# Sixty-two idle transposes in place of forty in the opening of a decoder-block kernel

## The chip, the core and the metric

The kernel runs on one core of a Trainium2 chip. The core has a matrix engine (TensorE, "PE" in the profile, its weight loads "PEld"), a vector engine (VectorE, "DVE"), a scalar engine (ScalarE, "ACT"), GpSimd ("POOL") and a sync engine that issues most transfers ("SP"). Each engine works through its own list of instructions in order; semaphores tie the lists together. The metric is the device time of one execution in microseconds, the median over several runs.

## The reference

One decoder layer on x of shape 1024 x 1024, in float32:

```python
u = rms_norm(h, mix_pre_g)
z = einsum('bsd,de->bse', u, w_in)               # p, q, k, v and two gates
ya = pool_mixer(p) @ w_branch_a                  # causal pooling, windows 2, 4, 8, 16
yb = diff_attention(q, k, v) @ w_branch_b        # 4 heads, two softmaxes each
m = sigmoid(gate_a) * ya + sigmoid(gate_b) * yb
h = h + rms_norm(m @ w_out, mix_post_g)
u = rms_norm(h, ffn_pre_g)
f = silu(u @ w_ffn_gate) * (u @ w_ffn_up)        # hidden width 2816
h = h + rms_norm(f @ w_ffn_down, ffn_post_g)
```

## The kernel before

All large products run on TensorE in a reduced float format. Each operand is split into a high part and a low part, and each product is three matmuls: high by high, low by high, high by low. The tiles of the activations are called `A_hi` and `A_lo` in the opening, those of the weights `w_hi` and `w_lo`. After the opening most products are done by a seven-product scheme on half matrices.

The work has four stages: the opening (normalising x and the first q and k products, up to about 80 us), the rest of the input projection, the attention and output projection, and the feed-forward part. Only the opening is touched by the change.

In the opening, x is loaded twice: by rows (tiles `xt`, eight blocks of 512 KB, line 344) for the sums of squares, and already transposed (tiles `xp` and `S_raw`, lines 349 and 353) as the operand of the products. ScalarE squares and sums each row block (line 389). For a group of two blocks VectorE adds the epsilon (line 397), GpSimd raises to the power -1/2 (line 398), and the result `rstd`, one value per row, has to become one value per column: two transposes on TensorE of a broadcast column (line 404, tile `R` in PSUM) do this, the "spreading" of 1/rms. ScalarE or VectorE copies `R` to SBUF (line 408). There are four such groups and so four spreadings. The transposed x is multiplied by the gain (lines 430 and 433), then by `R` (line 303, from `second_stage`), cast to `A_hi` (line 458), and the remainder is `A_lo` (line 1405). The weights are cast to `w_hi` (line 492), and the remainder is `w_lo` (line 1405). Then come the first products, `qk` (line 542), in pairs of matmuls with 256 moving columns.

Before x arrives TensorE has nothing to do. Line 318 issues 10 transposes of the identity matrix into a PSUM tile `warm` that nobody reads, as one task, and lines 320 to 322 issue 40 more, each a task of its own.

The order of the work within each engine of the opening is fixed by a planner in the kernel's own code (class `Plan`), when the program is built. Each task has an engine, a cost in us as its author wrote it, its tiles and a rank. The planner walks through planned time: on each engine it takes, among the tasks that can start at once, the one with the smallest rank. The idle transposes have rank 1,000,000, so one of them is put in only where no other TensorE task is ready in the plan. They are chained to each other since all write the tile `warm`. The plan fixes only the order; on the chip each instruction runs when the one before it on its engine and the semaphores it waits for allow it. TensorE starts in the plan at 1.42, the planner charges 0.11 when TensorE resumes after idling, and a result of GpSimd reaches TensorE 0.15 after its end, one of ScalarE 0.10 after its end.

Of the kernel before, what the change touches and what calls it, by code (L numbers as in the profile page):

```python
# [16 lines left out]
P = 128  # L17
# [226 lines left out]

AIM = 34.641
WARM0 = 10
WARM1 = 40
FORMS = (("DVE", "DVE", "DVE", "DVE",), ("DVE", "DVE", "DVE", "DVE",),)
WBEHIND = (0, None, 0, None,)
WSPLIT = (0, 1, 1, 0,)  # L250
# [30 lines left out]
def opening(pl, k):  # L281

    nc = k.nc if k else None
# [9 lines left out]
    def bank(pool, s):  # L293
        return pl.tile(pool, lambda: getattr(k, pool)(s))

    def small(n, s):
        return pl.tile("small", lambda: k.small(n, s))
# [11 lines left out]
    for g, w in enumerate(WINDOWS):  # L309
# [3 lines left out]
              w=[cnt], rank=-50)  # L313
# [3 lines left out]
    bw = bank("mm", "warm")  # L317
    pl.op("PE", WARM0 * .213, lambda: [nc.tensor.transpose(bw()[:, i % 4 * P:(i % 4 + 1) * P], k.ident, k.ident)
                                       for i in range(WARM0)], w=[bw], rank=-2000)
    for i in range(WARM1):  # L320
        pl.op("PE", .109, lambda i=i: nc.tensor.transpose(bw()[:, i % 4 * P:(i % 4 + 1) * P], k.ident, k.ident),
              w=[bw], rank=1e6)
    early = small(1, "early")
    pl.op("ACT", 1.3, lambda: A.copy(early(), k.mhalf[:, :1]), w=[early], rank=-2999)
    gk = small(KD, "gk")
# [44 lines left out]
    for c in LOADS:  # L370
        if c < 10:
            load_x(c)
        elif c < 20:
            i = c - 10
# [9 lines left out]
    for gi, grp in enumerate(GROUPS):  # L384
        n = len(grp)
        ss, r = small(n, "ss"), small(n, "rstd")
        for j, tb in enumerate(grp):
# [4 lines left out]
            else:  # L392
# [6 lines left out]
              rank=RT[gi], port=True)  # L399
# [84 lines left out]
    for i in range(4):  # L484
# [16 lines left out]
        else:  # L501
            pl.op("DVE", 1.23, lambda i=i: k.sub(wl[i](), view(i), wh[i]()), r=[raw[i], wh[i]],
                  w=[(wl[i], c) for c in range(4)], rank=WRANK[i] + 1, port=True)

    U = {"A11": AT[0, 0], "A12": AT[0, 1], "A22": AT[1, 1]}
    for n, raw_ in (("S1", s1), ("S2", r11), ("S3", s3), ("S4", r12)):
# [3 lines left out]
              rank=SRANK[n] + .5, port=True)  # L510
# [847 lines left out]
def block_kernel(ctx, tc, x, w_in, pool_mix, pool_scale, w_branch_a, lam_q1, lam_k1, lam_q2,  # L1358
# [203 lines left out]
    def qk_done(h, e, t, src, st):  # L1562
# [16 lines left out]
    lamt = temp("sg").rearrange("p (i d) -> p i d", d=HD)  # L1579
    first = Plan()  # L1580
    U, W, st = opening(first, SimpleNamespace(
        nc=nc, a8=a8, b4=b4, mm=mm, fil=fil, pair=pair, small=small, wp=wp, name=name, f32=f32, triple=triple, temp=temp,
        sub=sub, junk=junk, mhalf=mhalf, ident=ident, cnt=cnt, x=x, xt0=xt0, xt1=xt1, gk=gk, wqk=wqk, qd=qd, kd=kd, AF=AF))
# [393 lines left out]
```

## Time and profile before

| | us |
|---|---|
| median of 3 runs | 1244.17 (1243.64 to 1244.72) |
| the profiled execution, its own time | 1243.25 |
| span of the profiled execution | 1241.5 |
| TensorE busy | 1230.6 (99%) |
| VectorE busy | 842.7 (68%) |
| ScalarE busy | 584.2 (47%) |
| GpSimd busy | 127.8 (10%) |

The span runs from the first to the last instruction of the program; 1.75 us of the execution's own time lie around it. In a timeline row the first number is the start in us, the second how long the group lasted, then engine, line, operation, tiles, shape and count; in square brackets stands how long the engine had idled and what ended this. In a row of a table by stretches of time each engine has its busy time and its count of instructions, and "PEclk" is the granted share of the TensorE clock.

### The profile page before, as it was taken

The page shows a single profiled execution, that of the slowest core. Times are in us where ns is not written, and L with a number is a line of the kernel's source. Part 1 is how long each engine was busy: PE and PEld are TensorE (multiplying, and loading weights), DVE is VectorE, ACT ScalarE, POOL GpSimd, SP SyncE. Part 2 cuts the span into 40 slices and gives each one's busy share as a digit, 9 for nine tenths or more (in the row PEclk, how much of TensorE's full clock was granted, in tenths as well). Part 3 has the DMA queues.
Part 4 walks back from the last instruction along what each step waited for, and adds up shares of the span by engine and source line. Part 5 has one row for each costly group of instructions (what it writes and reads, how often), then busy time and mean ns, then how long its engine had stood idle before and what let it go on. Part 6 is the DMA issues. An engine that isn't in the chain of part 4 may idle for free.

```text
span 1241.5 us, 15579 instructions
## 1 busy us (share of the span) xinstructions
PE 1230.6 (99%) x5838; PEld 1033.0 (83%) x5838; DVE 842.7 (68%) x1307; ACT 584.2 (47%) x1049; POOL 127.8 (10%) x108
## 2 busy tenths in 40 slices
PE   8999999999999999999999999999999999999998
PEld 8888888888899998888888888888888888888886
DVE  6986784534599888886895564565655547955666
ACT  8643444443588773454643333333333333554542
POOL 1000000000201110011001111101111102000222
PEclk9999999999999999999999999999999999999999
DMA  9665346323783028562523232232332368733236
GB/s 372 234 196 185 108 152 226 124 80 118 289 321 136 18 86 290 195 243 94 191 89 120 93 127 102 94 102 95 117 127 86 125 215 276 233 103 100 81 106 212
DMA packets 133820, 194.36 MB, mean 157 GB/s; under 512 B 7920, under 2 KB 82416, under 8 KB 131312
## 3 DMA queue, kind: packets, MB, share of 16 engines
q1 hardware_dynamic: 126928, 172.26, 40.8%
q10 hardware_dynamic: 6816, 21.11, 4.4%
q8 instruction: 46, 0.75, 0.2%
q14 instruction: 30, 0.25, 0.1%
HBM read 131.73 MB, written 61.60 MB: 156 GB/s over the span
## 4 chain that ended last, share of the span: by engine, by line
PE 97%; DMA 1%; DVE 1%; ACT 0%; issue 0%; POOLq 0%; POOL 0%; DVEq 0%; ACTq 0%
PE Y L1498 10%; PE Y L1500 10%; PE Y L1499 10%; PE X L1498 5%; PE X L1500 5%; PE X L1499 5%; PE qk L542 4%; PE Yd L1498 3%; PE Yd L1500 3%; PE Yd L1499 3%; PE Z L1500 3%; PE Z L1498 3%; PE Z L1499 3%; PE s L710 3%; PE o L710 3%; PE wo L1500 2%
## 5 line engine op out<-in xcount | busy, mean ns | idle before, releaser
L1449 DVE TENSOR_TENSOR p<-Z,p 128x512 f32<-128x512 f32 x32 | 22.1, 691 | 160.7 <-PE Z L1500 160.7
L1498 PE MATMUL X<-S_hi,Wh 128*128 128x512 f32 x288 | 112.3, 390 | 0.0
L1498 PE MATMUL Y<-S_hi,Wh 128*128 128x512 f32 x288 | 112.2, 390 | 0.0
L1499 PE MATMUL Y<-S_lo,Wh 128*128 128x512 f32 x288 | 112.2, 389 | 0.0
L1500 PE MATMUL Y<-S_hi,Wl 128*128 128x512 f32 x288 | 112.1, 389 | 0.0
L1499 PE MATMUL X<-S_lo,Wh 128*128 128x512 f32 x288 | 112.1, 389 | 0.0
L1500 PE MATMUL X<-S_hi,Wl 128*128 128x512 f32 x288 | 112.0, 389 | 0.0
L1498 PE MATMUL Y<-A_hi,Wh 128*128 128x512 f32 x280 | 109.1, 390 | 0.0
L1499 PE MATMUL Y<-A_lo,Wh 128*128 128x512 f32 x280 | 109.1, 390 | 0.0
L1500 PE MATMUL Y<-A_hi,Wl 128*128 128x512 f32 x280 | 109.0, 389 | 0.0
L1467 ACT CAST Wh<-wf_t 128x1024 fp32r<-128x1024 f32 x62 | 64.3, 1052 | 64.1 <-PE Y L1499 32.8
L1405 DVE TENSOR_TENSOR Wl<-wf_t,Wh 128x1024 fp32r<-128x1024 f32 x72 | 87.6, 1223 | 6.1 <-ACT Wh L1467 4.6
L1405 DVE TENSOR_TENSOR w_op<-wd,w_op 128x512 fp32r<-128x512 f32 x77 | 56.6, 735 | 51.4 <-ACT w_op L1453 51.4
L1453 ACT CAST w_op<-wd 128x512 fp32r<-128x512 f32 x77 | 47.9, 622 | 78.0 <-PE Yd L1500 35.1
L1467 ACT CAST Wh<-w_raw 128x1024 fp32r<-128x1024 f32 (+1 forms) x62 | 51.9, 837 | 63.1 <-PE Z L1499 38.3
L1405 DVE TENSOR_TENSOR Wl<-w_raw,Wh 128x1024 fp32r<-128x1024 f32 x72 | 68.6, 953 | 15.0 <-ACT Wh L1467 13.6
L1498 PE MATMUL Yd<-w_op,s_op 128*128 128x512 f32 x176 | 68.6, 390 | 0.0
L1499 PE MATMUL Yd<-w_op,s_op 128*128 128x512 f32 x176 | 68.5, 389 | 0.0
L1500 PE MATMUL Yd<-w_op,s_op 128*128 128x512 f32 x176 | 68.3, 389 | 0.0
L1498 PEld LDWEIGHTS Y<-S_hi,Wh 128*128 128x128 f32 x288 | 54.1, 188 | 11.6 <-ACT u L1540 0.5
L1500 PEld LDWEIGHTS X<-S_hi,Wl 128*128 128x128 f32 x288 | 54.1, 188 | 11.2
L1500 PEld LDWEIGHTS Y<-S_hi,Wl 128*128 128x128 f32 x288 | 54.1, 188 | 11.2
(294 smaller groups left out, 3018.9 us busy)
## 6 DMA issues: line engine op xcount, KB each, us to landing
s_raw<-fsd SPq DMA_DIRECT2D x35, 512.0 KB, 3.5
w_raw<-in_w_in_dram SPq DMA_DIRECT2D x24, 512.0 KB, 4.0
w_raw<-in_w_ffn_gate_dram SPq DMA_DIRECT2D x22, 512.0 KB, 3.7
w_raw<-in_w_ffn_up_dram SPq DMA_DIRECT2D x22, 512.0 KB, 3.7
fsd<-fss SPq DMA_DIRECT2D x11, 1024.0 KB, 3.8
wd<-in_w_ffn_down_dram SPq DMA_DIRECT2D x44, 256.0 KB, 5.2
fsd<-F SPq DMA_DIRECT2D x33, 256.0 KB, 2.2
sgs<-sgd SPq DMA_DIRECT2D x16, 512.0 KB, 8.1
```

The source lines that it names most:

```text
L542: nc.tensor.matmul(o()[:, cs], l, r, start=first and kk == 2 * kh and j == 0, stop=last and kk == 2 * kh + 1 and j == len(todo) - 1, skip_ ...
L710: nc.tensor.matmul(o, l, r, start=start, stop=stop, skip_group_check=skip)
L1405: nc.vector.tensor_tensor(out=o, in0=a, in1=f32(hi), op=ALU.subtract)
L1449: nc.vector.tensor_tensor(out=o, in0=a, in1=b, op=op)
L1453: nc.scalar.copy(hi, a)
L1467: nc.scalar.copy(hi, a)
L1498: nc.tensor.matmul(o, ah, bh, start=start, stop=False, skip_group_check=goes_on)
L1499: nc.tensor.matmul(o, ah, bl, start=False, stop=False, skip_group_check=goes_on)
L1500: nc.tensor.matmul(o, al, bh, start=False, stop=stop, skip_group_check=goes_on)
```

## The change

The number of idle transposes after the first ten goes from 40 to 62. The planner's cost for the first 19 of them goes from 0.109 to 0.161, and each has a rank of its own, growing by one. Nothing else is edited; the planner places the transposes anew.

```diff
-WARM1 = 40
+WARM1 = 62
...
     for i in range(WARM1):
-        pl.op("PE", .109, lambda i=i: nc.tensor.transpose(bw()[:, i % 4 * P:(i % 4 + 1) * P], k.ident, k.ident),
-              w=[bw], rank=1e6)
+        pl.op("PE", .161 if i < 19 else .109, lambda i=i: nc.tensor.transpose(bw()[:, i % 4 * P:(i % 4 + 1) * P], k.ident, k.ident),
+              w=[bw], rank=1e6 + i)
```

## The prediction

> **What bounds the kernel.** I read first the page's busy times and its chain, then who TensorE waited for over the whole span.
>
> ```profile
> span 1241.5 us, 15579 instructions
> ...
> PE 1230.6 (99%) x5838; PEld 1033.0 (83%) x5838; DVE 842.7 (68%) x1307; ACT 584.2 (47%) x1049; POOL 127.8 (10%) x108
> ```
>
> ```profile
> PE qk L542 <- ACT A_hi L458: 2.9, 2, 1.8
> PE warm L318 <- POOL ident masks.py:199: 1.4, 1, 1.4
> PE branch L1498 <- DVE sgs L713: 0.2, 1, 0.2
> ```
>
> TensorE is the bound, and after its first products it waits for nothing but 0.2 us. So the end moves by what TensorE gains or loses in the opening, unless an operand there comes too late. The timeline of the first 21 us shows how the opening goes:
>
> ```profile
> 1.42 2.40 PE L318 MATMUL warm<-ident 128*128 128x128 f32 x10 [1.42 <-POOL ident masks.py:199]
> 3.60 6.20 PE L321 MATMUL warm<-ident 128*128 128x128 f32 x40
> 7.50 0.71 POOL L398 TENSOR_TENSOR rstd<-ms,mhalf 128x2 f32<-128x2 f32 x1 [5.85 <-DVE ms L397]
> 8.63 1.14 DVE L433 TENSOR_SCALAR A_raw<-xp,gk 128x256 f32<-128x256 f32 x4 [1.22 <-DMA xp<-in_xt_dram]
> 9.64 0.38 PE L404 MATMUL R<-ident,rstd 128*128 128x128 f32 x2
> 10.06 0.37 ACT L408 COPY R<-R 128x256 f32<-128x256 f32 x1 [1.01 <-PE R L404]
> 10.46 2.43 DVE L303 TENSOR_TENSOR A_raw<-A_raw,R 128x512 f32<-128x512 f32 x3 [0.69 <-ACT R L408]
> 11.19 1.22 ACT L458 CAST A_hi<-A_raw 128x512 fp32r<-128x512 f32 x2 [0.24 <-DVE A_raw L303]
> 11.86 1.11 PE L542 MATMUL qk<-A_hi,w_hi 128*128 128x256 f32 x4 [1.84 <-ACT A_hi L458]
> 12.98 1.04 ACT L458 CAST A_hi<-A_raw 128x1024 fp32r<-128x1024 f32 x1
> 14.07 1.22 PE L542 MATMUL qk<-A_hi,w_hi 128*128 128x256 f32 x4 [1.11 <-ACT A_hi L458]
> 16.44 1.22 DVE L1405 TENSOR_TENSOR A_lo<-A_raw,A_hi 128x1024 fp32r<-128x1024 f32 x1
> 17.82 1.08 POOL L398 TENSOR_TENSOR rstd<-ms,mhalf 128x2 f32<-128x2 f32 x1 [9.61 <-DVE ms L397]
> 18.14 3.30 ACT L430 ACTIVATE A_raw<-xp,gk 128x256 f32<-128x256 f32 x8
> 19.15 1.84 PE L542 MATMUL qk<-A_lo,w_hi 128*128 128x256 f32 x14
> 20.82 0.38 PE L404 MATMUL R<-ident,rstd 128*128 128x128 f32 x2
> ```
>
> Two things cost time here. The first spreading starts at 9.64, though its input was ready at 7.50 + 0.71 = 8.21: the idle transposes stand in front of it. And the clock falls, as the tables by stretches show (the first for the tile `warm` alone, the second for TensorE):
>
> ```profile
> 3.60:7.00 3.40, 3.40 (x17) 3.40 (x17) 1.00 1.01 396
> 7.02:9.60 2.58, 2.58 (x25) 2.54 (x24) 1.00 0.96 360
> ```
>
> ```profile
> 0.18:3.59 3.41, 2.17 (x10) 1.00 0.49 139
> 3.59:7.01 3.42, 3.42 (x18) 1.00 1.00 395
> 7.01:10.42 3.41, 3.01 (x28) 1.00 0.96 366
> 10.42:13.83 3.41, 1.01 (x4) 1.00 1.05 417
> 13.83:17.25 3.42, 3.17 (x15) 0.50 1.03 412
> 17.25:20.66 3.41, 3.41 (x30) 1.00 1.02 408
> ```
>
> Less the one that reaches in from before, 16 transposes start in 3.40 us (0.213 each) until 7.0, and 24 in 2.58 (0.108 each) after it: TensorE runs at half speed until 7.0, whatever PEclk says there. Between 13.83 and 17.25, one stretch of 3.42 us, the granted clock is 0.50, after a stretch in which TensorE was busy 1.01 of 3.41 us, and 15 matmuls start in it against 30 in the next.
>
> **The change part by part. Where the transposes go** follows from the planner's rule and the costs in the code; it is an order, not a time. In the plan 1/rms is ready for TensorE at 8.14: 0.76 for the issue of the second x block, 2 x 1.30 for two loads of 0.494 MB at 0.38, 2.40 latency, 1.25 for the square, 0.15 and 0.70 for lines 397 and 398, and 0.04, 0.09 and 0.15 for the hand-overs. The forty of before end in the plan at 1.42 + 2.13 + 40 x 0.109 = 7.91, all ahead of the spreading. Now nineteen end at 3.55 + 19 x 0.161 = 6.61, and 15 more start before 8.14 (the last at 8.135), so 34 stand ahead of the spreading, which ends at 8.244 + 0.218 = 8.462. The first pair of products is ready in the plan at 10.63, the second at 11.25, as before, since VectorE's earlier work and not `R` sets them. So (10.63 - 8.462) / 0.109 gives 20 transposes, then a pair (0.24), then 4, a pair, and the last 4, which end at 11.99; the third pair stays at 12.95. From there the plan is the old one, so no other order changes: 34, 20, 4 and 4.
>
> **The spreading.** Six fewer transposes ahead of it, all of them in the fast stretch: 6 x 0.109 = 0.66, so it starts at 8.98, still after 8.21. The copy of `R` moves from 10.06 to 9.40 and VectorE's product from 10.46 to 9.80; VectorE is free at 8.63 + 1.14 = 9.77, so all 0.66 pass. The casts after it move along, and the third pair goes from 14.07 to 13.41.
>
> **The 28 between.** They cost 28 x 0.109 = 3.05 us of TensorE, in time that was idle (9.86 to 11.86, and after the second pair). From 9.20 the 20 end at 11.38. The first pair is ready at about 11.80 - 0.66 + 0.05 = 11.19, and so 0.19 late; nobody waits for it but TensorE. Pair (0.24), 4 (0.44), pair, 4: they end at 12.74, 0.67 before the third pair is ready. Nothing on the path.
>
> **The clock.** From 10.42 to 13.83 TensorE is then busy 2.32 + 0.42 = 2.74 of 3.41 us, 80%, where 1.01 (30%) was followed by the half clock and 3.01 (88%) was not. I take it that the clock stays. Then 15 matmuls take 0.120 in place of 0.213: 15 x 0.093 = 1.40, and about 0.15 for the slower first ones. With it TensorE is 0.66 + 1.5 = 2.2 us ahead at 20.82. The bounds of this term are 0 (clock falls again) and 1.5. The operands of this part allow it: the last `A_lo`, 16.44 + 1.22 - 0.66 = 17.00, is wanted at 19.63 - 2.2 = 17.4, and 1/rms of the second group, at 18.90 - 0.66 = 18.24, at 18.6.
>
> **What is late next.** The timeline further on:
>
> ```profile
> 23.39 1.06 ACT L389 ACTIVATE junk<-xt 128x1024 bf16<-128x1024 f32 x1 [0.91 <-DMA xt<-in_x_dram]
> 24.67 1.06 ACT L389 ACTIVATE junk<-xt 128x1024 bf16<-128x1024 f32 x1
> 25.95 1.06 ACT L389 ACTIVATE junk<-xt 128x1024 bf16<-128x1024 f32 x1
> 27.01 1.03 ACT L458 CAST A_hi<-A_raw 128x1024 fp32r<-128x1024 f32 x1
> 28.07 1.22 DVE L1405 TENSOR_TENSOR A_lo<-A_raw,A_hi 128x1024 fp32r<-128x1024 f32 x1 [0.77 <-ACT A_hi L458]
> 28.46 0.38 PE L404 MATMUL R<-ident,rstd 128*128 128x128 f32 x2
> 28.60 0.72 PE L542 MATMUL qk<-A_hi,w_hi 128*128 128x256 f32 x4
> 29.16 0.38 PE L404 MATMUL R<-ident,rstd 128*128 128x128 f32 x2
> ```
>
> ```profile
> 25.00:28.40 3.40, 3.40 (x31) 1.00 1.03 410
> ```
>
> ScalarE waits for a block of x at 23.39, and the next two squares follow at 1.28 us, which is 512 KB at 410 GB/s: the transfers set these, and the change does not touch them. The cast of 27.01 stands behind the last square in ScalarE's list and ends at 28.04. Of the four matmuls of the row at 28.60, the last two (about 28.92) read its tile. So TensorE cannot pass 28.09 there, and of the 2.2 us only 28.92 - 28.09 = 0.83 is kept; some 1.4 us turn into a new wait for `A_hi`. After it TensorE is 0.83 ahead to the end. VectorE's `A_lo` at 28.07 doesn't move and ends at 29.29, wanted at 31.04 - 0.83.
>
> **The sum**, against the profiled execution: 1243.25 - 0.83 = 1242.42, of which 1241.5 - 0.83 = 1240.7 is span. The median of the runs is 0.92 above the profiled execution: 1244.17 - 0.83 = 1243.3. A difference of 0.2%, about what a measurement of this kernel can tell from no change, is 2.49 us here.
>
> **The rivals.** *No gain.* The clock's stretches are 3.41 us long, and one trace shows only one position of them. Where they lie so that no stretch is nearly idle, the kernel before keeps its full clock, reaches 28.09 by itself, and nothing is gained: 1244.2. The 1.08 us between the three runs speak for such differences; against it, the profiled execution had the half clock and was the fastest of the four. By the Trainium skill, "TensorE: Matmul & The Clock Gate", Part 1, the window is 3413 ns and free-running; the 3.41 of the trace agrees, a second position no run shows yet.
>
> *The transposes don't hold the clock.* Then 13.83 to 17.25 is at half clock again: from 13.41 four matmuls start fast and 16 slowly, 20 against 15, which is 5 x 0.120 = 0.60 ahead, below the 0.83: 1243.6. Against it speaks that the transposes' own spacing halved at 7.0, after a stretch of nothing else. The same page, Part 4, says of transposes that the full clock "doesn't engage" for them; by that rule the time would be this rival's, and the trace does not agree.
>
> *The full gain.* If the wait at 28.09 is not hard, 2.2 us remain: 1242.0. Only earlier transfers of x could do it; the row of 25.00 to 28.40 shows them at 410 GB/s without a pause.
>
> *Slower.* The new wait of 1.4 us, from 26.7 to 28.09, leaves 2.0 of 3.41 us busy (59%) if it lies within one stretch. If that is too little, the next 3.41 us go at half clock and cost 1.71: 1244.17 - 0.83 + 1.71 = 1245.05. It decides if the share at which the clock falls lies above 59%; the trace puts it between 30% and 88%. That 2.17 of 3.41 us (64%) from 0.18 to 3.59 did not raise the clock speaks for it. Against it: to fall and to rise need not have one limit.
>
> **How the numbers follow.** The forecast 0.55, no gain 0.12, the clock not held 0.08, the full gain 0.08, slower 0.12, and 0.05 for something else, such as an order that I worked out wrongly. The predicted time is 1243.3. The range takes in the full gain and the slower rival: 1242.0 to 1245.1. None of the named cases alone passes 2.49 us; faster by over 0.2% takes the full gain and a better position of the stretches (0.06), slower by over 0.2% takes the fallen clock and one more such loss, or the something else (0.07). That leaves 0.87 for within 0.2%.
>
> **What would show it.** In the profile of the changed kernel: the spreading of line 404 near 8.98 with 34 transposes of line 321 ahead of it and 28 behind; granted clock 1.00 from 13.83 to 17.25; the third pair near 13.41; a new wait of `qk` for `A_hi` of line 458 of about 1.4 us that ends near 28.1; the total of the waits of `qk` near 0.67 + 1.4. The prediction is wrong if TensorE's matmul after that wait starts earlier than 28.0 or if the clock falls after it, or if the order behind the third pair differs from before.

## The result, and the profile after

| us | before | changed |
|---|---|---|
| median, 22 runs each | 1244.03 (1242.42 to 1245.38) | 1242.01 (1241.38 to 1242.97) |
| the profiled execution, its own time | 1243.25 | 1242.02 |
| its span | 1241.5 | 1240.2 |

The ratio of the changed kernel to the one before is 0.9985, with a 95% interval of 0.9979 to 0.9991. That is within 0.2%, but it is a gain: 2.02 us between the medians, where 0.83 was forecast. Between the two profiled executions it is 1.23.

The page and the waits of TensorE in the changed kernel (engine, line, waited for: us in total, times, longest):

```profile
span 1240.2 us, 15622 instructions
...
PE 1231.4 (99%) x5860; PEld 1034.7 (83%) x5860; DVE 844.6 (68%) x1307; ACT 584.1 (47%) x1049; POOL 126.8 (10%) x108
```

```profile
PE warm L318 <- POOL ident masks.py:199: 1.4, 1, 1.4
PE qk L542 <- ACT A_hi L458: 1.0, 2, 0.5
PE branch L1498 <- DVE sgs L713: 0.2, 1, 0.2
```

TensorE has its 22 transposes more, and the wait for `A_hi` has shrunk from 2.9 to 1.0 us. Its timeline in the opening:

```profile
3.60 5.57 PE L321 MATMUL warm<-ident 128*128 128x128 f32 x34
9.01 0.38 PE L404 MATMUL R<-ident,rstd 128*128 128x128 f32 x2
9.23 2.35 PE L321 MATMUL warm<-ident 128*128 128x128 f32 x20
11.33 0.48 PE L542 MATMUL qk<-A_hi,w_hi 128*128 128x256 f32 x2
11.65 0.60 PE L321 MATMUL warm<-ident 128*128 128x128 f32 x4
12.01 0.48 PE L542 MATMUL qk<-A_hi,w_hi 128*128 128x256 f32 x2
12.33 0.60 PE L321 MATMUL warm<-ident 128*128 128x128 f32 x4
13.45 0.74 PE L542 MATMUL qk<-A_hi,w_hi 128*128 128x256 f32 x4 [0.52 <-ACT A_hi L458]
18.82 0.38 PE L404 MATMUL R<-ident,rstd 128*128 128x128 f32 x2
26.46 0.38 PE L404 MATMUL R<-ident,rstd 128*128 128x128 f32 x2
26.59 0.48 PE L542 MATMUL qk<-A_hi,w_hi 128*128 128x256 f32 x2
27.57 0.50 PE L542 MATMUL qk<-A_hi,w_hi 128*128 128x256 f32 x2 [0.49 <-ACT A_hi L458]
```

The order is 34, 20, 4 and 4. With the transposes left out, the order on all five engines is that of before. The third pair starts at 13.45 in place of 14.07, the second spreading at 18.82 in place of 20.82, and the pair at 28.92 now starts at 27.57 behind a new wait. TensorE by the clock's stretches (the columns: length, busy us and count of TensorE, PEclk, DMA share, GB/s):

```profile
10.48:13.89 3.41, 2.89 (x26) 1.00 1.05 420
13.89:17.30 3.41, 3.41 (x31) 1.00 1.03 410
```

In the stretch that was followed by the half clock TensorE is now busy 2.89 of 3.41 us, and the half clock is gone.

### The profile page after: what moved, and what is told of

The parts are those of the page before. It is cut to its first block, busy times and chain, and to the rows that moved or that the text cites. A ratio compares the mean times of both kernels' runs of the same rounds, so it can differ in the third digit from the quotient of the medians.

```text
span 1240.2 us, 15622 instructions
## 1 busy us (share of the span) xinstructions
PE 1231.4 (99%) x5860; PEld 1034.7 (83%) x5860; DVE 844.6 (68%) x1307; ACT 584.1 (47%) x1049; POOL 126.8 (10%) x108
## 4 chain that ended last, share of the span: by engine, by line
PE 95%; DMA 3%; DVE 1%; ACT 1%; SPq 0%; issue 0%; POOLq 0%; DVEq 0%; ACTq 0%
PE Y L1498 10%; PE Y L1499 10%; PE Y L1500 10%; PE X L1498 5%; PE X L1500 5%; PE X L1499 5%; PE Yd L1498 3%; PE Yd L1499 3%; PE Yd L1500 3%; PE Z L1500 3%; PE Z L1498 3%; PE Z L1499 3%; PE s L710 3%; PE o L710 3%; PE qk L542 3%; PE wo L1500 2%
```

## The experiments

### The kernel before, three times more

The kernel is unchanged; three more executions were profiled, to see where the clock's stretches lie.

> The kernel before, unchanged, looked at a second time. Theory A (the place of the clock's stretches): the stretches of 3.41 us begin elsewhere, so the first rise of the clock is not at 7.0 us, the first spreading does not start at 9.64 and the time of half clock, if there is one, does not begin at 13.83; the matmul pair at 28.92 moves with it, by up to a microsecond. Theory B (the loads): the clock changes at 7.0, 13.8 and 17.2 again, and only the landings of x differ, by a few tenths.

> The kernel before, unchanged, a third time. Theory A: again another place of the stretches, and the time goes with it: the later the clock rises, the longer the run, between 1242.5 and 1245.5. Theory B: as in the first look, within 0.5 us of 1243.3.

> The kernel before, unchanged, a fourth look for the place of the clock's stretches. The theory of the place says: the first rise of the clock anywhere between 4.8 and 8.3 us, the spreading at the earliest near 8.5 and at the latest near 10.2, and a half clock only where a whole stretch lies between about 9.9 and 14.1.

They took 1243.07, 1243.11 and 1244.58 us. The first rise of the clock comes at 6.62, 6.88 and 6.18 us; the stretches are always 3.41 us long, and they lie elsewhere in each execution. The longest, the third of them, by its stretches:

```profile
6.18:9.59 3.41, 3.41 (x31) 1.00 1.00 370
9.59:13.00 3.41, 1.03 (x5) 1.00 1.03 407
13.00:16.42 3.42, 2.75 (x13) 0.50 1.03 414
16.42:19.83 3.41, 3.41 (x18) 0.50 1.02 408
19.83:23.24 3.41, 3.41 (x30) 1.00 1.02 406
```

and the first of them:

```profile
10.03:13.45 3.42, 1.00 (x4) 1.00 1.05 416
13.45:16.86 3.41, 2.97 (x14) 0.50 1.02 408
16.86:20.27 3.41, 3.41 (x30) 1.00 1.03 412
```

The half clock can last two stretches, and this the forecast did not have. The third pair, which TensorE waits for, starts 0.44 us into the stretch of half clock in the first execution and 0.67 us into it in the third. Busy 2.97 of 3.41 us (87%), the clock rises behind the stretch; busy 2.75 (80%), it does not, and 3.41 us more go at half speed.

How far the opening has come is read from the first matmul of its last part, tile `Y`. The rows of the profiled execution before, of the third of the extra ones, and of the changed kernel:

```profile
60.51 0.39 PE L1498 MATMUL Y<-A_hi,Wh 128*128 128x512 f32 x1
```

```profile
61.43 0.39 PE L1498 MATMUL Y<-A_hi,Wh 128*128 128x512 f32 x1
```

```profile
59.26 0.39 PE L1498 MATMUL Y<-A_hi,Wh 128*128 128x512 f32 x1
```

The first and second extra executions of the kernel before have 60.23 and 60.43 here, two more executions of the changed kernel 59.26 and 59.55. Theory A holds in that the stretches move and the end of the opening moves with them. It named only one stretch, and so its sentence that a late rise makes a long run is wrong: the execution with the earliest rise was the longest. The fall in it also comes behind a stretch that begins at 9.59, a little ahead of the 9.9 that was expected.

The runs below complete the picture. Seven profiles have the gap unfilled: four of the kernel before, and one each with the earlier spreading alone, with the shortened loads and with the cast moved. The four in which the clock first rises at 4.14, 4.92, 5.26 and 6.18 us have two stretches of half clock, and the three with 6.62, 6.88 and 7.00 have one.

### The changed kernel, twice more

> The changed kernel, unchanged, a second time. Theory A: wherever the stretches lie, TensorE is stopped by the same cast of ScalarE, so the pair that was at 27.57 us starts within 0.6 us of that, after a wait of 0.3 to 1.5 us. Theory B: the pair follows the landing of the last x block, about 2.2 us after it.

> The changed kernel, unchanged, beside the two on the same chip: 0.1 to 0.2% below the kernel before, and in its profile no half clock before the last microseconds, with the pair behind the wait near 27.56 us once more, wherever the stretches lie.

The first took 1241.72 us. Its clock rises at 5.53, the first spreading is at 8.26 in place of 9.01, and the pair starts at 27.56, where 27.57 was seen, after a wait of 0.78 us. The second was timed beside the kernel before on one chip: 1242.39 against 1243.91, a ratio of 0.9987 (0.9978 to 0.9996); rise at 7.17, pair at 27.86 after 0.75 us. Neither has a half clock before the last microseconds. In these three executions the end of the opening does not follow the stretches: TensorE comes early and waits. They do not tell theory A from theory B, though. The last row block of x lands at 25.34, 25.34 and 25.64 us in them, 2.2 us ahead of the pair each time, as theory B has it too. The shortened loads below decide.

### The earlier spreading alone

```diff
-WARM1 = 62
+WARM1 = 40
```

> The changed kernel with 40 idle transposes in place of 62: 34 stand ahead of the first spreading and 6 behind it, so the spreading is as early as in the changed kernel, and the gap before the first products is left nearly empty. If the earlier spreading alone makes the gain (0.66 us, with the wait for the cast as the limit): 1242.0 to 1242.6, nearly all of the gain. If the held clock makes it: the clock falls for 3.41 us near 13.8, and the time is 1243.2 to 1243.8, a third of the gain or less.

1243.16 us against 1243.89, a ratio of 0.9996 (0.9987 to 1.0005): no difference that can be told. The profile shows the spreading at 8.04 (the stretches lie early here), and the gap:

```profile
8.04 0.43 PE L404 MATMUL R<-ident,rstd 128*128 128x128 f32 x2
8.31 0.82 PE L321 MATMUL warm<-ident 128*128 128x128 f32 x6
10.86 1.18 PE L542 MATMUL qk<-A_hi,w_hi 128*128 128x256 f32 x4 [1.74 <-ACT A_hi L458]
13.08 1.23 PE L542 MATMUL qk<-A_hi,w_hi 128*128 128x256 f32 x4 [1.03 <-ACT A_hi L458]
```

```profile
8.33:11.75 3.42, 1.58 (x12) 1.00 1.04 393
11.75:15.16 3.41, 2.38 (x11) 0.50 1.03 420
15.16:18.57 3.41, 3.41 (x17) 0.50 1.02 408
```

The third pair comes at 13.08, and two stretches at half clock eat what was won: the first `Y` is at 60.54, where the kernel before had 60.23 to 61.43.

### The filling alone

```diff
-WARM1 = 62
+WARM1 = 68
...
-        pl.op("PE", .161 if i < 19 else .109, lambda i=i: nc.tensor.transpose(
+        pl.op("PE", .1148 if i < 40 else .109, lambda i=i: nc.tensor.transpose(
```

> 68 idle transposes, 40 of them ahead of the first spreading, as in the kernel before, and 28 behind it, 21 of these before the first pair of products. So the spreading stays at 9.64 and only the gap is filled. If the held clock makes the gain: no half clock after 13.8, TensorE about 1.5 us ahead at 20.8 until it waits for the cast, 1242.0 to 1242.6. If the earlier spreading makes it: 1243.5 to 1244.2.

1241.84 us against 1243.46, a ratio of 0.9988 (0.9979 to 0.9997); the order is 40, 21, 4 and 3. That is the changed kernel's gain within the intervals. The profile has no half clock before the last microseconds. Its first spreading is not at 9.64 but at 8.63, since the clock rose at 4.94 in this execution. That happens to be the place of the stretches in the profile of the earlier spreading alone, where it rose at 4.92, so the two can be compared directly. The first and second spreading here, and the second of the other:

```profile
8.63 0.38 PE L404 MATMUL R<-ident,rstd 128*128 128x128 f32 x2
18.44 0.38 PE L404 MATMUL R<-ident,rstd 128*128 128x128 f32 x2
```

```profile
20.86 0.38 PE L404 MATMUL R<-ident,rstd 128*128 128x128 f32 x2
```

With the filling the first spreading is 0.59 us later (8.63 for 8.04) and the second 2.42 us earlier. The pair then waits 0.75 us for `A_hi` and starts at 28.02. The held clock makes the gain. Whether the earlier spreading adds anything to it can't be told within these intervals; TensorE waits for the cast with it and without it.

This run also bears on the forecast's slower rival. The new waits lie within one stretch, and TensorE is busy 2.35 of its 3.41 us (69%):

```profile
25.42:28.83 3.41, 2.35 (x19) 1.00 1.02 408
28.83:32.25 3.42, 3.42 (x31) 1.00 1.04 412
```

The clock stays. It fell behind stretches with 1.00 to 1.58 us busy (29% to 46%). The 59% of the rival lie between and were reached in no run.

### What sets the new wait

The forecast put it down to the landing of the last row blocks of x. ScalarE in the changed kernel:

```profile
17.64 1.71 ACT L430 ACTIVATE A_raw<-xp,gk 128x256 f32<-128x256 f32 x4
20.26 1.71 ACT L430 ACTIVATE A_raw<-xp,gk 128x256 f32<-128x256 f32 x4 [0.91 <-DMA xp<-in_xt_dram]
21.88 1.04 ACT L389 ACTIVATE junk<-xt 128x1024 bf16<-128x1024 f32 x1
23.04 1.06 ACT L389 ACTIVATE junk<-xt 128x1024 bf16<-128x1024 f32 x1
24.23 1.06 ACT L389 ACTIVATE junk<-xt 128x1024 bf16<-128x1024 f32 x1
25.43 1.06 ACT L389 ACTIVATE junk<-xt 128x1024 bf16<-128x1024 f32 x1
26.48 1.03 ACT L458 CAST A_hi<-A_raw 128x1024 fp32r<-128x1024 f32 x1
```

The squares follow each other at 1.16 to 1.20 us and wait for nothing; ahead of them ScalarE waits for a block of the transposed x. But the row blocks are close: the last one lands at 25.34, only 0.09 us ahead of its square. To take them out of it, the last four were loaded for a quarter of their columns in both kernels (the diff is shortened):

```diff
-        ... nc.sync.dma_start(xt[tb](), k.x[tile_cols(tb), :]) ...
+        ... nc.sync.dma_start(xt[tb]()[:, :256] if tb > 3 else xt[tb](), k.x[tile_cols(tb), :256] if tb > 3 else k.x[tile_cols(tb), :]) ...
...
-        A.activation(k.junk, xt[tb](), ...
+        A.activation(..., xt[tb]() if tb < 4 else xt[tb]()[:, :256].rearrange("p (o c) -> p o c", o=1).to_broadcast([P, 4, 256]), ...
```

> The kernel before, with the last four row blocks of x loaded for a quarter of their columns only; their squares read that quarter four times, so ScalarE works as long (the norms of those rows are not the reference's). It takes 1.5 MB out of the loads. TensorE waits for no load in the kernel before, so if the landings of x only stop the faster kernel: within 0.3 us of the kernel before, 1243.8 to 1244.3. If the loads stop the kernel before as well in most of its runs: a gain of 0.5 us or more.

> The changed kernel with the same cut of the loads. If the landings of x set the cast that TensorE waits for near 27.6: the wait goes, TensorE stays about 2.2 us ahead, and the time is 0.7 to 1.4 below the changed kernel, 1240.6 to 1241.3. If something else sets it: 1242.0 as the changed kernel, with the wait in its place.

The kernel before with the cut: 1243.88 us against 1243.46, a ratio of 1.0003 (0.9993 to 1.0012), no difference that can be told, as expected. The changed kernel with the cut: 1241.88, a ratio of 0.9987 (0.9978 to 0.9996), about the gain of the changed kernel. The interval alone would leave room for some tenths more; the rows decide. Its ScalarE:

```profile
20.17 1.71 ACT L430 ACTIVATE A_raw<-xp,gk 128x256 f32<-128x256 f32 x4 [0.86 <-DMA xp<-in_xt_dram]
21.78 1.04 ACT L389 ACTIVATE junk<-xt 128x1024 bf16<-128x1024 f32 x1
...
25.32 1.06 ACT L389 ACTIVATE junk<-xt 128x1024 bf16<-128x1024 f32 x1
...
26.37 1.03 ACT L458 CAST A_hi<-A_raw 128x1024 fp32r<-128x1024 f32 x1
```

With three quarters of these loads gone the squares run at the same pace, the cast comes 0.11 us earlier (0.09 of it since the transposed x landed at 20.15 and not at 20.24), and TensorE still waits 0.66 us for it. So in the changed kernel the row blocks do not set the wait, though they come no more than some hundredths ahead of what does. From 20.26 on ScalarE's own list does: four gains, four squares and the cast, 7.25 us to the cast's end; and its start hangs on one landing of the transposed x. In the three profiles of the changed kernel and in this one the pair starts 7.3 us behind that landing (20.24, 20.22, 20.53 and 20.15 us).

### The cast ahead of the last square

```diff
-               ... rank=R + OFF[4], port=e == "DVE")
+               ... rank=R + OFF[4] - (20 if (n, q) == (1, 1) else 0), port=e == "DVE")
```

> The changed kernel with the rank of one cast lowered by 20 (line 458, the one of 128x1024 that ScalarE does behind its fourth-last square and its last three). The planner then puts it ahead of the last square, and the fourth spreading on TensorE some 1.2 us later in its plan. If ScalarE's own list sets the wait of 0.65 to 0.94 us near 27.5 in the changed kernel: the cast ends near 26.3, the wait goes or shrinks to 0.2, and the time is 0.5 to 0.9 below the changed kernel's. If a landing sets it: the wait stays within 0.2 us, and the time with it.

> The kernel before with the same cast ahead of the last square. TensorE comes there late, 0.9 us behind the cast, in all looks at the kernel before. If the half clock is all that it loses to the changed kernel: no difference to the kernel before, within 0.4 us, and at least one stretch of half clock. If the cast limits it in some executions: 0.3 to 0.8 us faster.

Both theories missed. On the changed kernel it took 1244.92 us against 1243.91 for the kernel before (ratio 1.001, 1.0001 to 1.0019), and on the kernel before 1246.68 (1.0024, 1.0014 to 1.0034). The cast does come earlier, at 25.57, but the planner reorders TensorE around it. The waits of the first of the two:

```profile
PE qk L542 <- ACT A_hi L458: 2.2, 3, 1.0
...
PE qk L542 <- DVE qk_st L1405: 1.1, 1, 1.1
PE Y L1498 <- DVE p L1449: 0.6, 1, 0.6
```

The products that read this tile now stand further ahead on TensorE and wait for it all the same (0.97 us), and three waits further on are new: 1.1 us that ends at 41.26, 0.6 that ends at 43.53, and 0.6 for `p` behind the opening. In the second run the first products already wait 3.3 us where the kernel before has 1.8. So the runs show what one rank moves in such a plan; they do not test the wait by itself, and no version faster than the changed kernel came of them.

## Why the prediction was right or wrong

The changed kernel's time lies in the range, and a change within 0.2% was forecast and measured. That the time lies in the range is luck: 1242.01 is 0.01 us inside its lower end, and that end is the price of a rival, the full gain, that did not come. The order, the spreading, the filling and the clock came as worked out: 34, 20, 4, 4; 9.01 for 8.98; the third pair 13.45 for 13.41; busy 2.89 us for 2.74 in the stretch; full clock after it; TensorE 2.00 ahead at the second spreading for 2.2.

Wrong was the size of the gain, 2.02 us for 0.83, by two steps: 0.40 us of the difference lies between the two profiled executions (1.23 for 0.83), and 0.79 between the profiled executions and the medians. By the prediction's own sign, a start after the wait earlier than 28.0, its account of that wait is wrong.

The first is "What is late next": "TensorE cannot pass 28.09 there, and of the 2.2 us only 28.92 - 28.09 = 0.83 is kept". The pair started at 27.57, so 1.35 is kept there between the two profiled executions, and 1.25 at the first `Y`. The wait is there, of 0.5 us and not 1.4, and in the place named, but 28.09 was the bound of one execution only. In the profile of before the last square of a row block starts at 25.95. In the three other executions of the same kernel it starts at 25.70, 25.61 and 25.45; the last of these:

```profile
25.45 1.06 ACT L389 ACTIVATE junk<-xt 128x1024 bf16<-128x1024 f32 x1
```

In the three of the changed kernel it starts at 25.43, 25.42 and 25.72. So the landings scatter by half a microsecond with nothing changed, and the one execution that the forecast read was the latest of the four. And in the changed kernel ScalarE's own list ends as late as the landings allow, to within a tenth: with the row blocks cut short the wait is still there.

The second is the price of the half clock, which the forecast took from the one position of the stretches that it saw. The sum added the gain of the profiled executions to the median of the runs, though the profiled execution before lies 0.78 us below the median of its kernel (1243.25 against 1244.03) and the changed one at its own (1242.02, 1242.01). The opening of before ends 0.7 to 1.3 us behind the changed kernel's with one stretch (60.23 to 60.51 against 59.26 to 59.55), and 1.9 to 2.2 us behind it with two (61.43). The profiled execution before had one, with the latest rise of the seven. That two stretches in other executions make up the 0.78 is likely, but not shown. How often one stretch falls and how often two was not counted, since the mean clock also holds what falls after the last product; and on another chip the medians differ by 1.52 us, so part of the 2.02 may be scatter. The rival "No gain" had the same root with the sign turned round: I thought that some positions spare the kernel before. No profile shows one. The mean granted clock was 0.996 to 0.998 in each of its 67 executions timed beside the experiments, and 0.998 to 1.000 in all 22 of the changed kernel. In 43 of the 67 it was 0.997 or less, which takes over 6 us of half clock; behind the last product the profiles have at most 4.1 us of it. The other 24, at 0.998, it can't decide: the profile of the filling alone has 0.998 with no half clock in the opening.

The other rivals: the transposes do hold the clock, as the filling alone shows. By the Trainium skill, "TensorE: Matmul & The Clock Gate", Part 4, the full clock does not engage for transposes; these runs don't agree, with 0.50 before and 1.00 after 28 of them are put into the gap. The free-running window of 3413 ns that the Trainium skill gives on that page (Part 1) they do show now: first rises at 5.53, 6.18, 6.62, 6.88, 7.00, 7.07 and 7.17 us, and 3.41 us for each stretch. The full gain did not come, since the wait for the cast is real. The slower rival's price needed a clock that falls at 59% busy. With the shorter wait the stretch that holds most of it was busy 2.95 of 3.41 us (86%) in the changed kernel's profile, and at 69%, the least that a run had there, the clock stayed; 59% stays open.

## What to carry to other kernels

Idle matmuls are worth their time where TensorE has a short piece of work inside a longer pause: what counts is its busy share in each stretch of the clock, and here pauses of 1.8 and 1.1 us with two pairs of matmuls between cost one or two stretches at half speed. One profile shows one position of these stretches, so price such a pause by the mean over positions, from several profiles, before adding it to a median. The same holds for a landing: one profile shows one time of it. And ask of the wait that comes next which of its several inputs is close behind the last one: with three quarters of the last row blocks' loads gone, the cast came only 0.11 us earlier.

## What was not expected of the hardware

The clock does not simply come back after one stretch: TensorE busy 80% of a stretch at half clock left it there for the next, 87% raised it. The busy share by itself does not give the limit, since one stretch at the start, of the kernel before with the cast moved (0.73 to 4.14, busy 2.72 us, 80%), did raise the clock. And the landings jump: the second transposed block of x landed 1.0 us later in the changed kernel (20.24 for 19.21), behind a transfer of instructions. The DMA queues of the changed kernel from 17.7 to 19.7, and of the kernel before in the same time (queue, kind: packets, MB, share of 16 engines):

```profile
q1 hardware_dynamic: 224, 0.79, 99.6%
q8 instruction: 1, 0.02, 3.4%
```

```profile
q1 hardware_dynamic: 227, 0.82, 102.4%
```

In the kernel before the same packet, about 1.1 us on one of the sixteen engines, comes at 20.85, and there the landings have a gap of 2.8 us (20.50 to 23.31) where 1.28 is usual. With the loads back to back, one packet on one engine seems to delay all that lands after it. All thirteen profiles have one such gap between 12 and 29 us, of 2.4 to 2.8 us, and in all of them the packet starts within 0.6 us of the gap's beginning. The packet comes earlier in the kernels in which TensorE is ahead: it starts at 20.58 to 20.85 us in the four profiles of the kernel before, at 18.05 to 18.22 in the three of the changed one, and at 16.80 with the filling alone, where ScalarE waits for the transposed x until 19.13 and the pair starts at 28.02. So with TensorE ahead the gap falls on an earlier block, here on the one on which the cast's list hangs. That the two go together is what the traces show; that the one causes the other was not tested.
